# Gated tiles of layer 1 made final in DRAM in paced steps; output stage in another order of heads

## The chip, the cores and the metric

The kernel runs on one core of a Trainium2 chip. Its time is the device time of one execution in microseconds (us); the time of a kernel is the median of its runs. A profile is one execution taken apart by the hardware profiler. TensorE (PE) multiplies matrices, VectorE (DVE), ScalarE (ACT) and GpSimd (POOL) work on tiles, and SyncE (SP) issues most of the DMAs, in the order of its queue.

## What is computed

A decoder trunk of two layers on 1024 tokens of width 1024. Layer 0 is retention, layer 1 differential attention with 16 heads. In each, a branch of width 2048 is gated and projected back to 1024 columns, normalized and added. For the change only the end of layer 1 matters:

```python
attn = probs[:, :, 0] - lam * probs[:, :, 1]          # per head, causal, with a relative bias
out  = einsum('bhqk,bhke->bhqe', attn, v)             # 16 heads of 128 columns
out  = rmsnorm(out, subln_g, eps=GN_EPS) * (1.0 - lambda_init)   # over the 128 columns of a head
y    = out.transpose(0, 2, 1, 3).reshape(B, S, 2048)
gated = silu(g) * y
x    = x + rmsnorm(gated @ w_out, post_norm_g)        # w_out: 2048 x 1024
```

So each output row of a head is scaled by one number, its 1/rms over the head's 128 columns.

## The kernel before

Tokens are in eight blocks of 128. Every matrix product is done as three products of a high and a low part (names with h and l), which is why each matmul line stands three times. A tile that feeds TensorE is therefore made in steps: a load from DRAM (raw), a cast on ScalarE (h), a subtraction of the cast from the original (l) on VectorE or GpSimd.

**Attention of layer 1** walks through 16 heads x 8 query blocks in 128 steps. In between, a stream of filler matmuls (projections of later heads, whose weights `load_w` loads through SP's queue into two raw buffers and splits with ScalarE and GpSimd, line 83) fills TensorE. TensorE's order is written by hand there; the other engines' and SP's orders are made by a scheduler from a simulated timeline, and every engine keeps its order. `values` makes the output of a head for two token blocks, multiplied by the gate (heads 0 to 11) but not yet by 1/rms, and ScalarE's queue stores it in the DRAM tensor g1. `square_sum` stores the sums of squares (ssd). `row_scales` turns them, with the softmax sums s0all that TensorE transposes (line 834), into the 1/rms rows rsd. It runs twice: for heads 0 to 11 in head 12, and for heads 12 to 15 at the very end. For the four late heads the gate is stored apart (sgd).

**Output stage of layer 1** (`output_stage`). For each half of the 1024 output columns and each token block, the sixteen heads are accumulated in one PSUM bank: 16 x 3 matmuls of 128x512. A gated tile comes from `gated8` (eight heads) or from the inner `gated` (four heads): load from g1, load of the 1/rms rows spread over the partitions (w_rb, rsb), multiplication on GpSimd (lines 108, 472), cast on ScalarE (111, 475), subtraction on VectorE (112, 476); in the last four heads also the gate (sgl, line 471). WIDE says how many of the four quarters come from `gated8`: two in each half. Blocks 0 and 1 have heads 0 to 11 of the first half done within attention, as filler; blocks 2, 3 and 4 get them while the last scales are made. After the first half of a block, two tiles of the second half's weights are loaded over the slots (`load_out`). In the second half each block's row is normalized, added to x1d and stored.

`rsqrt` is a Newton iteration on VectorE that begins with a shift and a multiplication.

Of the kernel before, what the change touches and what calls it, by code (L numbers as in the profile page):

```python
# [10 lines left out]
F32 = mybir.dt.float32  # L11
F32R = mybir.dt.float32r
I32 = mybir.dt.int32
# [6 lines left out]
P = 128  # L20
T = 1024
# [14 lines left out]
WIDE = ((4, 4), (2, 2))  # L36
# [5 lines left out]
BSPLIT = 12  # L42
# [8 lines left out]
class _Trunk:  # L51
# [7 lines left out]
    def rsqrt(self, out, v, n, tag, np_=P, t=None, hv=None):  # L59
# [35 lines left out]

    def gated8(self, layer, parts):
        nc = self.nc
        gsrc = self.g0 if layer == 0 else self.g1
        raw = self.wp.tile([P, 8, P], F32, tag="raw", name="w_raw", bufs=2)
        rb = self.wp.tile([P, 8, P], F32, tag="raw", name="w_rb", bufs=2) if layer == 1 else None  # L100
# [350 lines left out]
    def output_stage(self, layer, slots, nextR, prologue, head):  # L451
        nc, io = self.nc, self.io
        gsrc = self.g0 if layer == 0 else self.g1
        with ExitStack() as es:
            ptr = self.pool(es, "fpst", PSUM)
            ptr.tile([P, 4, P], F32, tag="T", name="ps_t", bufs=2)
# [3 lines left out]
            def gated(tb, kq):  # L460
                raw = fp.tile([P, 4, P], F32, tag="graw", name="graw", bufs=3)
                nc.sync.dma_start(raw, gsrc[tb, :, kq * 4:kq * 4 + 4, :])
                if layer == 1:
                    rb = fp.tile([P, 4, P], F32, tag="rsb", name="rsb", bufs=2)
                    b, k0 = (0, kq * 4) if kq * 4 < BSPLIT else (1, kq * 4 - BSPLIT)
                    nc.sync.dma_start(rb, self.rsd[b][tb:tb + 1, k0:k0 + 4, :].broadcast_to([P, 4, P]))
                    if kq == 3:
                        n = DH - LATE
                        sg = fp.tile([P, n, P], F32, tag="sgl", name="sgl")
                        nc.sync.dma_start(sg, self.sgd[tb])  # L470
                        nc.vector.tensor_mul(raw[:, 4 - n:, :], raw[:, 4 - n:, :], sg)  # L471
                    nc.gpsimd.tensor_mul(raw, raw, rb)  # L472
# [576 lines left out]
```

## Time and profile before

| | |
|---|---|
| median of 3 runs | 2211.82 us (2211.01 to 2216.42) |
| profiled execution, its own time | 2212.31 us |
| its span | 2210.5 us |
| mean granted TensorE clock | 0.991 |
| busy: PE, DVE, ACT, POOL | 2145.4, 1325.3, 852.8, 471.0 us |
| DMA | 181.30 MB, mean 82 GB/s |

Attention of layer 1 ends at about 2012 us, the output stage of layer 1 at the span's end. A busy TensorE is one whose modelled matmuls overlap without a gap; the granted clock says at which of its two levels it ran (1.0 is 2.4 GHz). A wait is the idle time of an engine before an instruction, with the instruction that released it.

### The profile page before, as it was taken

How to read it: one execution, taken by the hardware profiler on the slowest of the kernel's cores; microseconds unless marked ns; L12 is line 12 of the kernel's file. 1: busy time of each engine (PE TensorE's matmuls, PEld its weight loads, DVE VectorE, ACT ScalarE, POOL GpSimd, SP SyncE). 2: the span in 40 equal slices, each digit the busy share in tenths (PEclk: the TensorE clock that was granted, in tenths of full speed). 3: DMA queues.
4: the chain of work that ended last, by engine and by line, in shares of the span. 5: the costliest groups of instructions: out<-in, count | busy, mean ns of one | idle time of the engine just before them, and what ended most of it. 6: DMA issues, size and time to landing. Idle time of an engine off the chain costs nothing. (4 is left out here: it accounts for less than half of the span.)

```text
span 2210.5 us, 31034 instructions
## 1 busy us (share of the span) xinstructions
PE 2145.4 (97%) x11860; PEld 1798.2 (81%) x11860; DVE 1325.3 (60%) x3158; ACT 852.8 (39%) x1648; POOL 471.0 (21%) x260
## 2 busy tenths in 40 slices
PE   7999999999999999999999999999999999998997
PEld 7888988888897888787888888887887888776775
DVE  5264344344436348556776676676676776774765
ACT  4121221221122333345455554555545565542421
POOL 2322411501521000211111111111111111123651
PEclk9999999999999999999999999999999999999999
DMA  4112212112123544311111111111111111145874
GB/s 165 61 39 74 61 35 68 44 50 72 44 72 95 191 153 171 101 41 39 51 39 32 47 50 39 40 50 39 38 40 42 48 41 39 63 136 183 280 251 158
DMA packets 95430, 181.30 MB, mean 82 GB/s; under 512 B 8433, under 2 KB 50609, under 8 KB 95153
## 3 DMA queue, kind: packets, MB, share of 16 engines
q1 hardware_dynamic: 60368, 162.31, 22.6%
q10 hardware_dynamic: 34912, 17.01, 2.5%
q8 instruction: 93, 1.52, 0.3%
q14 instruction: 57, 0.46, 0.1%
HBM read 151.86 MB, written 30.56 MB: 83 GB/s over the span
## 5 line engine op out<-in xcount | busy, mean ns | idle before, releaser
L83 POOL TENSOR_TENSOR w_l<-w_raw,w_h 128x1024 fp32r<-128x1024 f32 x112 | 271.5, 2429 | 1332.1 <-ACT w_h L82 1325.3
L762 ACT ACTIVATE e<-ps_s,nm 128x896 f32<-128x896 f32 (+7 forms) x256 | 189.8, 742 | 105.4 <-DVE nm L760 93.8
L216 PE MATMUL ps_mm<-RB,w_h 128*128 128x512 f32 x512 | 209.5, 409 | 0.3 <-ACT RB L151 0.3
L158 PE MATMUL ps_mm<-RA,w_h 128*128 128x512 f32 x512 | 203.7, 398 | 1.6 <-DVE sg L427 1.6
L159 PE MATMUL ps_mm<-RA,w_h 128*128 128x512 f32 x512 | 204.9, 400 | 0.0
L217 PE MATMUL ps_mm<-RB,w_h 128*128 128x512 f32 x512 | 201.9, 394 | 1.0 <-DVE RB L152 1.0
L218 PE MATMUL ps_mm<-RB,w_l 128*128 128x512 f32 x512 | 202.7, 396 | 0.0
L160 PE MATMUL ps_mm<-RA,w_l 128*128 128x512 f32 x512 | 202.3, 395 | 0.0
L789 ACT CAST ath<-ps_t 128x512 fp32r<-128x512 f32 (+1 forms) x192 | 91.8, 478 | 217.3 <-PE ps_t L786 211.9
L757 DVE TENSOR_REDUCE mx<-ps_s 128x1 f32<-128x640 f32 (+2 forms) x192 | 119.4, 622 | 82.3 <-PE ps_s L732 78.0
L82 ACT CAST w_h<-w_raw 128x1024 fp32r<-128x1024 f32 x112 | 117.6, 1050 | 121.0 <-PE ps_mm L159 33.4
L648 PE MATMUL ps_mm<-w_h,RB 128*128 128x256 f32 x512 | 147.7, 289 | 0.0
L170 PE MATMUL ps_mm<-w_h,RA 128*128 128x256 f32 x512 | 145.8, 286 | 0.0
L168 PE MATMUL ps_mm<-w_h,RA 128*128 128x256 f32 x512 | 145.0, 285 | 0.8 <-ACT RA L151 0.8
L169 PE MATMUL ps_mm<-w_l,RA 128*128 128x256 f32 x512 | 145.1, 284 | 0.1
L650 PE MATMUL ps_mm<-w_h,RB 128*128 128x256 f32 x512 | 143.8, 281 | 0.0
L649 PE MATMUL ps_mm<-w_l,RB 128*128 128x256 f32 x512 | 143.8, 281 | 0.0
L111 ACT CAST g_h<-w_raw 128x1024 fp32r<-128x1024 f32 x50 | 52.5, 1049 | 183.8 <-POOL w_raw L108 81.1
L158 PEld LDWEIGHTS ps_mm<-RA,w_h 128*128 128x128 f32 x512 | 96.2, 188 | 25.2 <-DVE sg L427 2.3
L218 PEld LDWEIGHTS ps_mm<-RB,w_l 128*128 128x128 f32 x512 | 96.2, 188 | 23.6
L112 DVE TENSOR_TENSOR g_l<-w_raw,g_h 128x1024 fp32r<-128x1024 f32 x50 | 71.3, 1427 | 73.0 <-ACT g_h L111 71.0
L160 PEld LDWEIGHTS ps_mm<-RA,w_l 128*128 128x128 f32 x512 | 96.2, 188 | 22.0
(217 smaller groups left out, 5520.9 us busy)
## 6 DMA issues: line engine op xcount, KB each, us to landing
w_raw<-in_wn SPq DMA_DIRECT2D x64, 512.0 KB
w_raw<-g SPq DMA_DIRECT2D x48, 512.0 KB
w_raw<-in_wv SPq DMA_DIRECT2D x32, 512.0 KB
w_raw<-in_wo SPq DMA_DIRECT2D x32, 512.0 KB
xt<-in_x SPq DMA_DIRECT2D x16, 512.0 KB
w_raw<-in_wg SPq DMA_DIRECT2D x16, 512.0 KB
g<-go ACTq DMA_DIRECT2D x32, 256.0 KB
g<-go ACTq DMA_DIRECT2D x64, 128.0 KB
```

Of the source, the lines that this page charges most:

```text
L83: nc.gpsimd.tensor_sub(l, raw, _f32(h))
L158: nc.tensor.matmul(ps, wh[:, k], region[:, kt, cols], start=(kt == 0), stop=False)
L159: nc.tensor.matmul(ps, wh[:, k], region[:, 8 + kt, cols], start=False, stop=False)
L160: nc.tensor.matmul(ps, wl[:, k], region[:, kt, cols], start=False, stop=(kt == KT - 1))
L168: nc.tensor.matmul(ps, region[:, kt, cols], wh[:, k], start=(kt == 0), stop=False)
L169: nc.tensor.matmul(ps, region[:, kt, cols], wl[:, k], start=False, stop=False)
L170: nc.tensor.matmul(ps, region[:, 8 + kt, cols], wh[:, k], start=False, stop=(kt == KT - 1))
L216: nc.tensor.matmul(ps, wh[:, k], HR[:, kt, tok], start=(kt == 0), stop=False)
L217: nc.tensor.matmul(ps, wh[:, k], HR[:, 8 + kt, tok], start=False, stop=False)
L218: nc.tensor.matmul(ps, wl[:, k], HR[:, kt, tok], start=False, stop=(kt == KT - 1))
L648: nc.tensor.matmul(ps[:, t, :], HR[:, kt, cols], wh[:, k], start=(kt == 0), stop=False)
L762: nc.scalar.activation(e[:, 0:n], S[:, 0:n], AF.Exp, bias=nm, accum_out=(s0 if m == 0 else s1))
```

## The change

Heads are now in three batches (0 to 7, 8 to 11, 12 to 15), each with its own DRAM tensors for the unscaled tiles (g1r), the sums and the scales; `row_scales` runs at heads 8, 12 and the end. After each of the first two, eight steps later, `finish` takes one quarter of a token block per attention step: it loads the unscaled tile and its scale rows through SP, multiplies on GpSimd, and the next step stores the final tile in g1f. That is 16 + 8 = 24 steps. A scheduling dependency ties their DMAs to a transpose of the step. In the output stage tiles of heads 0 to 11 are loaded final. The last four heads are finished there in the first half, by the old way, and stored for the second half. The first half now goes over heads 0 to 11 of all blocks in pairs, then over heads 12 to 15 of all blocks; six PSUM banks instead of four hold the sums. The second half takes all tiles from `gated8`. In `rsqrt` two lines change places.

```diff
-WIDE = ((4, 4), (2, 2))
+WIDE = ((4, 4), (2, 4))
-BSPLIT = 12
+BATCHES = ((0, 8), (8, 12), (12, 16))
...
+        nc.vector.tensor_scalar(out.bitcast(I32), v.bitcast(I32), 1, None, op0=ALU.arith_shift_right)
         nc.vector.tensor_scalar(hv, v, -0.5, None, op0=ALU.mult)
-        nc.vector.tensor_scalar(out.bitcast(I32), v.bitcast(I32), 1, None, op0=ALU.arith_shift_right)
...
+    def gsrc(self, layer, tb, kt, n):
+        if layer == 0:
+            return self.g0[tb, :, kt:kt + n, :]
+        return self.g1f[kt // 8][tb, :, kt % 8:kt % 8 + n, :]
...
         for tb, kt, n in parts:
-            nc.sync.dma_start(raw[:, o:o + n, :], gsrc[tb, :, kt:kt + n, :])
-            if layer == 1:
-                nc.sync.dma_start(rb[:, o:o + n, :], self.rsd[0][tb:tb + 1, kt:kt + n, :].broadcast_to([P, n, P]))
+            nc.sync.dma_start(raw[:, o:o + n, :], self.gsrc(layer, tb, kt, n))
             o += n
-        if layer == 1:
-            nc.gpsimd.tensor_mul(raw, raw, rb)
...
-            def gated(tb, kq):
+            def gated(tb, kq, hf):
                 raw = fp.tile([P, 4, P], F32, tag="graw", name="graw", bufs=3)
-                nc.sync.dma_start(raw, gsrc[tb, :, kq * 4:kq * 4 + 4, :])
-                if layer == 1:
+                if layer == 1 and kq == 3 and hf == 0:
+                    nc.sync.dma_start(raw, self.g1r[2][tb])
+                    sg = fp.tile([P, 4, P], F32, tag="sgl", name="sgl")
+                    nc.sync.dma_start(sg, self.sgd[tb])
                     rb = fp.tile([P, 4, P], F32, tag="rsb", name="rsb", bufs=2)
...
+                    nc.sync.dma_start(rb, self.rsd[2][tb:tb + 1].broadcast_to([P, 4, P]))
+                    nc.vector.tensor_mul(raw, raw, sg)
                     nc.gpsimd.tensor_mul(raw, raw, rb)
+                    nc.sync.dma_start(self.gsrc(1, tb, 12, 4), raw)
+                else:
+                    nc.sync.dma_start(raw, self.gsrc(layer, tb, kq * 4, 4))
...
-                return psm.tile([P, 512], F32, tag="mm", name="ps_mm", bufs=4)
+                return psm.tile([P, 512], F32, tag="mm", name="ps_mm", bufs=4 if layer == 0 else 6)
...
+                for tb in range(2, TB, 2):
+                    two = (tb, tb + 1)
+                    g = [self.gated8(1, ((t, 0, 8),)) for t in two]
+                    head += [bank() for t in two]
+                    for t in two:
+                        for _ in self.out_mm(head[t], g[t - tb], slots[0], 0, 8):
+                            pass
+                    g8 = self.gated8(1, tuple((t, 8, 4) for t in two))
+                    for t in two:
+                        for _ in self.out_mm(head[t], g8, slots[0], 8, 4, 4 * (t - tb)):
+                            pass
+                    second_half(tb - 2)
+                second_half(TB - 2)
+                for tb in range(TB):
                     product(head[tb], 0, tb, 3)
                     first(tb, head[tb])
+                lead = TB
...
+            def after(dma):
+                self.tc.add_manual_dep(dma.ins, mark["pe"].ins.name, mybir.DependencyInfo(mybir.DependencyClass.NoSync, mybir.DependencyReason.DATA), reason="paced")
+
+            def finish_store():
+                if held:
+                    dst, raw = held.pop()
+                    after(nc.sync.dma_start(dst, raw))
+
+            def finish(tb, h0):
+                b, hh, nh = batch(h0)
+                finish_store()
+                raw = wk.tile([P, 4, P], F32, tag="fraw", name="fraw")
+                rb = wk.tile([P, 4, P], F32, tag="frb", name="frb")
+                after(nc.sync.dma_start(raw, self.g1r[b][tb, :, hh:hh + 4, :]))
+                after(nc.sync.dma_start(rb, self.rsd[b][tb:tb + 1, hh:hh + 4, :].broadcast_to([P, 4, P])))
+                nc.gpsimd.tensor_mul(raw, raw, rb)
+                held.append((self.gsrc(1, tb, h0, 4), raw))
...
                 if rows is not None:
                     row_scales(*rows)
+                    todo += [None] * 8 + [(tb, h0) for h0 in range(*BATCHES[rows[0]], 4) for tb in range(TB)] + [()]
                     rows = None
+                elif todo:
+                    step = todo.pop(0)
+                    if step:
+                        finish(*step)
+                    elif step == ():
+                        finish_store()
```

Three places of the built orders show what moved. The first is SP's queue around heads 9 and 10, where weights (w_raw) for the filler are loaded; bt is a head's bias. Before:

```order
L79 DMA w_raw_15246<-in_wn1 128x1024
L79 DMA w_raw_15398<-in_wn1 128x1024
L79 DMA w_raw_15586<-in_wn1 128x1024
L716 DMA bt_15751<-xd_89 128x256
L79 DMA w_raw_15683<-in_wn1 128x1024
L79 DMA w_raw_15885<-in_wn1 128x1024
```

After, from the first of the same weight loads on (g1r0 holds the unscaled tiles of heads 0 to 7, g1f0 the final ones):

```order
L79 DMA w_raw_15321<-in_wn1 128x1024
L731 DMA fraw_14543<-g1r0_80 128x512
L732 DMA frb_14544<-rsd0_90 128x512
L724 DMA g1f0_83<-fraw_14543 128x512
L732 DMA frb_14612<-rsd0_90 128x512
L731 DMA fraw_14611<-g1r0_80 128x512
L79 DMA w_raw_15485<-in_wn1 128x1024
L724 DMA g1f0_83<-fraw_14611 128x512
L732 DMA frb_14710<-rsd0_90 128x512
L731 DMA fraw_14709<-g1r0_80 128x512
L724 DMA g1f0_83<-fraw_14709 128x512
```

Between two weight loads there now stand the stores and loads of finishing steps; a store waits for GpSimd's multiplication, and the next load of fraw for that store, since fraw has one buffer.

The second is SP's queue in the second half of the output stage, one token block's worth (w_raw is an 8-head tile, w_rb, rsb its scales, graw a 4-head tile, sgl the late gate, xt the residual). Before:

```order
L103 DMA w_raw_20434<-g1_80 128x1024
L462 DMA graw_20364<-g1_80 128x512
L470 DMA sgl_20389<-sgd_82 128x512
L105 DMA w_rb_20435<-rsd12_85 128x1024
L466 DMA rsb_20387<-rsd4_86 128x512
L466 DMA rsb_20469<-rsd12_85 128x512
L564 DMA out_0<-xt_20019 128x512 x2
L103 DMA w_raw_20537<-g1_80 128x1024
L462 DMA graw_20385<-g1_80 128x512
L546 DMA xt_20225<-x1d_81 128x1024
```

After:

```order
L106 DMA w_raw_20409<-g1f1_84 128x1024
L548 DMA xt_20291<-x1d_85 128x1024
L106 DMA w_raw_20464<-g1f0_83 128x1024
L566 DMA out_0<-xt_20206 128x512 x2
L106 DMA w_raw_20494<-g1f1_84 128x1024
```

A token block's eight loads, xt among them, are three, and what is loaded is multiplied by no scale any more.

The third is ScalarE in the last steps of head 15 (e is an exponential of the softmax, ath the copy of a transposed tile that the product with v needs, g_h the cast of a gated tile for the output stage). Before:

```order
L762 ACTIVATE e_19185,s0all_7687<-ps_s_19164,nm_19181 128x768
L808 ACTIVATE sq_19214<-ps_o_19207 128x256
L809 CAST sqh_19215<-sq_19214 128x256
L820 DMA g1_80<-go_19220 128x2x128
L762 ACTIVATE e_19192,s1_19179<-ps_s_19165,nm_19188 128x768
L111 CAST g_h_19347<-w_raw_19342 128x1024
L789 CAST ath_19071<-ps_t_19240 128x4x128
L789 CAST ath_19071<-ps_t_19253 128x2x128
```

After:

```order
L785 ACTIVATE e_19346,s0all_7693<-ps_s_19325,nm_19342 128x768
L110 CAST g_h_19505<-w_raw_19503 128x1024
L831 ACTIVATE sq_19375<-ps_o_19368 128x256
L785 ACTIVATE e_19353,s1_19340<-ps_s_19326,nm_19349 128x768
L832 CAST sqh_19376<-sq_19375 128x256
L844 DMA g1r12_82<-go_19381 128x2x128
L812 CAST ath_19232<-ps_t_19401 128x4x128
L110 CAST g_h_19562<-w_raw_19559 128x1024
L812 CAST ath_19232<-ps_t_19414 128x2x128
```

The cast that stood before both ath copies now stands between them, and it is that of a later tile.

## Rows read from the trace of the kernel before

**Rows 1.** Stretches: bounds, length, busy us (instructions) by engine, PEclk, DMA share, GB/s.
```profile
960.00:1900.00 940.00, 930.23 (x5518) 779.33 (x5517) 659.09 (x1758) 493.14 (x1058) 139.14 (x57) 1.00 0.14 43
...
2034.00:2060.00 26.00, 21.59 (x79) 16.61 (x80) 12.27 (x11) 8.17 (x12) 14.04 (x9) 0.85 0.83 258
```

**Rows 2.** Line 834, TensorE: min/median/max ns, first and last start us, forms.
```profile
L834 PE MATMUL ps_t<-ident,s0all x2: 270/292/313, 1752.7 to 2012.7; 128*96 128x128 f32 x1, 128*32 128x128 f32 x1
```

**Rows 3.** Timeline of TensorE in the output stage: start us, us, engine, line, operation.
```profile
2048.01 0.40 PE L125 MATMUL ps_mm<-RB,gl 128*128 128x512 f32 x1
...
2052.68 0.40 PE L124 MATMUL ps_mm<-RB,gh 128*128 128x512 f32 x1
...
2058.19 0.63 PE L124 MATMUL ps_mm<-RB,gh 128*128 128x512 f32 x1
2058.62 0.63 PE L125 MATMUL ps_mm<-RB,gl 128*128 128x512 f32 x1
...
2201.76 0.39 PE L125 MATMUL ps_mm<-RA,gl 128*128 128x512 f32 x1
```

**Rows 4.** Waits of TensorE, 2012 to 2211: us in total, times, longest.
```profile
PE ps_mm L125 <- DVE gl L476: 14.3, 8, 4.1
PE ps_mm L123 <- ACT g_h L111: 2.8, 1, 2.8
```

**Rows 5.** GpSimd by line, 2012 to 2211: busy us, mean ns, idle before, releasers.
```profile
L472 POOL TENSOR_TENSOR graw<-graw,rsb 128x512 f32<-128x512 f32 x28 | 41.8, 1506 | 47.1 <-DVE nv L559 16.7 <-DVE graw L471 14.8 <-DMA rsb<-rsd 6.0
L108 POOL TENSOR_TENSOR w_raw<-w_raw,w_rb 128x1024 f32<-128x1024 f32 x13 | 32.4, 2492 | 43.0 <-DMA w_rb<-rsd 37.3 <-DVE gl L476 5.0 <-DMA graw<-g 0.7
```

**Rows 6.** VectorE by line, 2012 to 2211.
```profile
L471 DVE TENSOR_TENSOR graw<-graw,sgl 128x512 f32<-128x512 f32 x16 | 22.1, 1382 | 44.6 <-DMA graw<-g 40.4 <-DMA sgl<-sgd 2.4 <-issue 1.8
L112 DVE TENSOR_TENSOR g_l<-w_raw,g_h 128x1024 fp32r<-128x1024 f32 x13 | 20.6, 1585 | 5.7 <-ACT g_h L111 5.7
```

**Rows 7.** Chain that ended last: start us, us, piece (DMA: issue to landing).
```profile
2027.91 1.85 DMA rsd<-rsr
2029.78 3.24 DMA rsb<-rsd
...
2047.18 6.91 DMA graw<-g
...
2096.77 7.74 DMA w_rb<-rsd
...
2184.19 2.08 DMA out<-xt
```

**Rows 8.** Timeline at the end of attention, ScalarE and TensorE; in brackets the wait.
```profile
2003.01 1.05 ACT L111 CAST g_h<-w_raw 128x1024 fp32r<-128x1024 f32 x1 [3.79 <-POOL w_raw L108]
...
2005.98 0.44 PE L786 MATMUL ps_t<-ident,e 128*128 128x128 f32 x2 [1.66 <-DVE atl L790]
```

**Rows 9.** Waits of TensorE in the attention, 960 to 1900.
```profile
PE ps_t L786 <- DVE e L768: 4.4, 6, 1.7
PE ps_o L801 <- DVE nm L760: 1.8, 3, 0.8
PE ps_t L834 <- DVE atl L790: 1.4, 1, 1.4
```

**Rows 10.** GpSimd by line in the attention, 960 to 1900.
```profile
L83 POOL TENSOR_TENSOR w_l<-w_raw,w_h 128x1024 fp32r<-128x1024 f32 x57 | 139.1, 2443 | 816.1 <-ACT w_h L82 816.1
```

**Rows 11.** Timeline in the attention, SP's queue and GpSimd.
```profile
1485.04 19.63 SPq L79 DMA_DIRECT2D w_raw<-in_wn  x3
...
1501.92 2.39 POOL L83 TENSOR_TENSOR w_l<-w_raw,w_h 128x1024 fp32r<-128x1024 f32 x1 [12.77 <-ACT w_h L82]
```

**Rows 12.** Timeline at the end of attention, GpSimd and VectorE.
```profile
1981.04 2.40 POOL L108 TENSOR_TENSOR w_raw<-w_raw,w_rb 128x1024 f32<-128x1024 f32 x1 [5.59 <-DVE mx L759]
1981.18 2.54 DVE L810 TENSOR_TENSOR sql<-sq,sqh 128x256 fp32r<-128x256 f32 x1
...
1997.76 0.42 DVE L810 TENSOR_TENSOR sql<-sq,sqh 128x256 fp32r<-128x256 f32 x1
```

More of the change, by code (lines that the diff above doesn't have):

```diff
@@ L484, in product, with second_half @@
                     return
-                for _ in self.out_mm(ps, gated(tb, kq), slots[hf], kq * 4, 4):
+                for _ in self.out_mm(ps, gated(tb, kq, hf), slots[hf], kq * 4, 4):
                     pass
             def bank():
-                return psm.tile([P, 512], F32, tag="mm", name="ps_mm", bufs=4)
+                return psm.tile([P, 512], F32, tag="mm", name="ps_mm", bufs=4 if layer == 0 else 6)
             acc = {}
+            def second_half(t0):
+                for t in (t0, t0 + 1):
+                    self.load_out(layer, slots, 1, t, fp.tile([P, D], F32, tag="x", name="w_raw", bufs=2))
             def first(tb, ps):
@@ L504, in first @@
                 nc.vector.tensor_mul(acc["y"][:, tb, :], ps, acc["postg"][:, 0:512])
-                if tb % 2 == 0:
-                    for t in (tb, tb + 1):
-                        self.load_out(layer, slots, 1, t, fp.tile([P, D], F32, tag="x", name="w_raw", bufs=2))
+                if layer == 0 and tb % 2 == 0:
+                    second_half(tb)
             if layer == 0:
@@ L708, in batch @@
             def batch(h):
-                return (0, h, BSPLIT) if h < BSPLIT else (1, h - BSPLIT, DH - BSPLIT)
+                return next((b, h - h0, h1 - h0) for b, (h0, h1) in enumerate(BATCHES) if h < h1)
             bts = {}
+            held = []
+            mark = {}
+            def after(dma):
[13 more added lines that the diff above has]
+                held.append((self.gsrc(1, tb, h0, 4), raw))
             def load_bias(h):
@@ L785, in attn_t @@
                 for kb in range(k0, k1):
-                    nc.tensor.transpose(out=tp[:, kb - k0, :], in_=A[:, kb * P:(kb + 1) * P], identity=self.ident)
+                    mark["pe"] = nc.tensor.transpose(out=tp[:, kb - k0, :], in_=A[:, kb * P:(kb + 1) * P], identity=self.ident)
                 clk["pe"] += (k1 - k0) * 0.109
@@ L896, in attention_layer @@
                     ready_o = clk["pe"] + SLACK["sq"]
-                    if i == ORDER[-1] and h == BSPLIT - 1:
+                    if i == ORDER[-1] and h + 1 in (BATCHES[0][1], BATCHES[1][1]):
                         fill_until(ready_o)
@@ L900, in attention_layer @@
                         pend = None
-                        rows = (0,)
+                        rows = (batch(h)[0],)
                 n_ = s + 1
@@ L910, in attention_layer @@
                 square_sum(*pend)
-            row_scales(1)
+            assert not todo and not held
+            row_scales(2)
             return heads
@@ L930, in run @@
         self.g0 = self.dr.tile([TB, P, NE, P], F32, name="g0")
-        self.g1 = self.dr.tile([TB, P, NE, P], F32, name="g1")
+        self.g1r = [self.dr.tile([TB, P, h1 - h0, P], F32, name="g1r%d" % h0) for h0, h1 in BATCHES]
+        self.g1f = [self.dr.tile([TB, P, 8, P], F32, name="g1f%d" % k) for k in range(2)]
         self.x1d = self.dr.tile([T, D], F32, name="x1d")
         self.sgd = self.dr.tile([TB, P, DH - LATE, P], F32, name="sgd")
-        self.ssd = [self.dr.tile([TB, n, P], F32, name="ssd%d" % n) for n in (BSPLIT, DH - BSPLIT)]
-        self.rsd = [self.dr.tile([TB, n, P], F32, name="rsd%d" % n) for n in (BSPLIT, DH - BSPLIT)]
+        self.ssd = [self.dr.tile([TB, h1 - h0, P], F32, name="ssd%d" % h0) for h0, h1 in BATCHES]
+        self.rsd = [self.dr.tile([TB, h1 - h0, P], F32, name="rsd%d" % h0) for h0, h1 in BATCHES]
         a, b = (lambda i: RA[:, i, :]), (lambda i: RB[:, i, :])
```

41 lines of the change are left out of this document (9 added, 32 removed).

## The prediction

> **What bounds the kernel now.** I read the stretches by engine first [rows 1]. In the attention of layer 1 (960 to 1900 us) TensorE is busy for 930 of 940 us at full granted clock: nothing can be won there, and everything added there must stay hidden. In the output stage it loses ground: from 2034 us it is busy for 21.6 of 26 us, at a granted clock of 0.85, with a DMA share of 0.83. So that is the place to look at.
>
> How much is there to win? The stage has 8 blocks x 2 halves x 16 heads x 3 = 768 matmuls. 72 of them (blocks 0 and 1, heads 0 to 11, first half) are done in the attention; 696 follow the transposition of line 834 at 2012.7 us [rows 2]. Undisturbed they start 0.234 us apart (20 steps from 2048.01 to 2052.68) [rows 3]: 696 x 0.234 = 162.9 us. The last ends at 2201.76 + 0.39 = 2202.15 [rows 3], after 189.4 us. **26.5 us are lost.** The waits name most of them: 14.3 us in 8 waits for gl and 2.8 us for g_h [rows 4]. The rest comes behind such waits: after the longest, the matmuls start 0.43 us apart (2058.19, 2058.62) [rows 3], which is TensorE at the lower of its two levels, 1.2 instead of 2.4 GHz.
>
> Why does gl come late? Every gated tile is loaded, its 1/rms rows are loaded beside it (rsb, w_rb), GpSimd multiplies, ScalarE casts, VectorE subtracts; and each tile is made twice, once for each half of the output columns. GpSimd alone spends 41.8 + 32.4 us on that after 2012 us, and stands 37.3 us before w_rb [rows 5]. VectorE stands 40.4 us at line 471, in its order, until graw lands [rows 6].
>
> **The second half (384 matmuls).** All tiles now come final from DRAM. Gone per token block are two rsb loads, one w_rb, one sgl and two graw, three GpSimd multiplications and one VectorE multiplication; left are two 8-head tiles, xt and the output. A tile serves 24 matmuls, 5.6 us. Making one takes a load of at most 7.74 us [rows 7], a cast of 1.05 us [rows 8] and a subtraction of 1.59 us [rows 6]: 10.4 us, over two raw buffers 5.2 us a tile, even in before's traffic. I expect no wait here.
>
> **The first half (312 matmuls after 2012.7).** TensorE has 216 matmuls (heads 0 to 11 of blocks 2 to 7), 50.5 us, before it needs the last scales, at about 2063 us. They are in DRAM at 2027.91 + 1.85 = 2029.8 us [rows 7]. If the VectorE work that now stands inside their chain (a weight subtraction, a tile, a product) adds 5 us, 28 us are still spare. What is late next is the last four heads: eight blocks of 12 matmuls, 2.8 us each. sgl has a single buffer there, so a block costs at least a load of 3.24 to 6.91 us [rows 7] and a multiplication of 1.38 us [rows 6]: 4.6 to 8.3 us. The order has the first four sgl loads ahead of TensorE's arrival. The other four fall behind by 4 x 1.8 to 4 x 5.5 = 7.2 to 22 us, less the three blocks that three graw buffers hold ready, 8.4 us. That gives 0 to 13.6 us; I take **+3**, near the low end, since the traffic behind the 6.91 us is what the change removes.
>
> **End of attention.** ScalarE, in order, stood 3.79 us in front of the cast at 2003.01 until GpSimd's multiplication was done, and TensorE lost 1.66 us at 2005.98 behind it [rows 8]. The multiplication is gone, and the cast now stands behind the first of the two ath copies; but it still stands before the last one and waits there for TensorE to free a buffer. Bounds -4 (this wait, the slow matmuls behind it, and a like wait before) and +2; I take **-2**.
>
> **A third pass over the scales,** at head 8. The pass at head 12 shows a TensorE wait of 1.4 us [rows 9]. Bounds 0 and 3; I take **+1.5**.
>
> **The 24 paced steps** put 72 DMAs on SP's queue and 24 multiplications on GpSimd's, in order, before weight loads and w_l subtractions of heads 8 to 14. GpSimd first: in 940 us it spent 139.1 us on 57 subtractions [rows 10], and TensorE's three longest rows of waits for VectorE are 4.4 + 1.8 + 1.4 = 7.6 us [rows 9]. If all of it came from GpSimd, 24 x 1.5 us [rows 5] = 36 us more cost 36 x 7.6 / 139.1 = 2 us. I take **+2**, bounds 0 and 6. Now SP. A step is a store, the loads, a multiplication, in series: 2.08 + 3.24 [rows 7] + 1.5 [rows 5] + 1 us for three issues = 7.8 us, or 11.5 us with a load of 6.91. Attention goes on by a step in (2012.7 - 1752.7) / 32 = 8.1 us (the two dates of line 834 lie 32 steps apart [rows 2]). So SP just keeps up. What hides a delay: the load issued at 1485.04 is subtracted at 1501.92 [rows 11], 16.9 us later; less at most 6 us to land and 1.05 us of cast, 10 us are spare for a weight tile. I cost the queue at nothing.
>
> VectorE and GpSimd hinder each other: sql, 0.42 us at 1997.76, took 2.54 us at 1981.18, beginning 0.14 us after a GpSimd multiplication and ending when that had ended [rows 12]. The Trainium skill ("SBUF — State Buffer", section "SBUF: two separate sides") has the rule for it: the port pair that the two engines share is an exclusive lock, held for a whole instruction, if the VectorE operation reads two SBUF inputs. The trace agrees in this row. By that rule the change carries the lock into the softmax, at worst 24 times; that case is the third rival below.
>
> **Layer 0** differs by two VectorE lines of rsqrt that changed places; the scheduler then orders some retention matmuls otherwise. 0, bounds -2 and +2.
>
> **Sum.** -26.5 + 3 - 2 + 1.5 + 2 = -22.0 us. Against the profiled execution's own 2212.31 us (span 2210.5) this is 2190.3 us; that execution lies 0.5 us above the median of 2211.82, so **2190 us**.
>
> **Rivals.** (1) The output stage stays bound by its feed. For it: the DMA share of 0.83 [rows 1], the single sgl buffer, VectorE's standing in its order before graw [rows 6]. The far end of the last four heads costs 13.6 instead of 3 us: 2201 us. Against it: most loads of scales and products are gone. (2) The step chain on SP is too slow, and weight tiles come late. At 10.1 us a step the sixteen steps of the first batch fall behind by 16 x 2.0 = 32 us; less the 10 us spare TensorE loses 22 us, the gain is gone: 2212 us. From 10.5 us a step on (16 x 2.4 - 10 = 28) the kernel is over 0.3% slower than before; at 11 us it takes 2226 us. Against it: the long loads were measured at 258 GB/s, attention moves 43 GB/s [rows 1]. (3) Each new GpSimd multiplication pushes the softmax by its 1.5 us, and TensorE with it: 36 instead of 2 us, 2224 us. Against it: 57 longer ones cost at most 7.6 us. (4) The change does less than it says: the added scheduling dependency on a transpose leaves no wait of SP on TensorE in the built order, so steps may bunch. SP then runs them as fast as its queue allows, one after another between weight loads; that costs nothing by itself, and its bad end is rival 2.
>
> **Chances.** The forecast, 2182 to 2197 us: 0.70. Rival 1, 2197 to 2204: 0.15. Better than 2182 (all terms at their good ends): 0.04. Rival 2 at about 10 us a step, no change: 0.06; beyond 10.5 us: 0.03. Rival 3: 0.02. A difference under 0.3%, 6.6 us, can't be told from none. Faster 0.89, same 0.06, slower 0.05. The range leaves out the better end, rivals 2 and 3: **2182 to 2204 us**.
>
> **What would show it.** In the profile after: no waits for gl or g_h in the first 50 us of the output stage and in its second half, and a granted clock of 1.0 there; the last four heads with waits of a few us in all, for gl, in blocks 4 to 7; finishing steps about 8 us apart or less and no TensorE wait for w_h or w_l in heads 8 to 14; the last matmul about 22 us earlier. Waits for w_h or w_l would show rival 2; more waits for nm, e or atl in heads 8 to 14, rival 3; long waits for gl late in the first half, rival 1. Each would make the prediction wrong.

## The result, and the profile after

The changed kernel takes **2182.3 us** (median of 4 runs, 2179.4 to 2183.9) against 2212.8 us before (4 runs beside them): ratio 0.9859, 95% interval 0.9842 to 0.9876, a gain of 30 us by the medians and 31 by the ratio. Run again later it took 2182.35 us (2181.7 to 2185.0), ratio 0.9861 (0.9845 to 0.9877). The forecast was 2190 us, a gain of 22. The direction and the main place were right; 8 to 9 us of the gain were not foreseen, and the time lies at the low end of the range, or by the ratio (0.9859 x 2211.82 = 2180.6 us) just below it.

The profiled execution of after took 2179.38 us (span 2177.6), which is 3 us below its median; before's lay at its own. The top of the page, busy time and share by engine:

```profile
PE 2132.8 (98%) x11861; PEld 1790.8 (82%) x11861; DVE 1283.4 (59%) x3155; ACT 851.6 (39%) x1638; POOL 429.3 (20%) x246
```

**The output stage** did what was forecast. Stretches in after (bounds, length, busy us by engine, PEclk, DMA share, GB/s), to be held against the second of [rows 1]:

```profile
2030.00:2060.00 30.00, 30.00 (x130) 24.16 (x129) 15.60 (x14) 11.77 (x14) 14.77 (x7) 1.00 0.87 293
2060.00:2090.00 30.00, 27.95 (x118) 21.57 (x118) 13.39 (x19) 8.29 (x21) 4.54 (x3) 1.00 0.45 139
2090.00:2120.00 30.00, 30.00 (x130) 24.16 (x129) 17.28 (x47) 7.90 (x12) 0.00 (x0) 1.00 0.49 168
```

TensorE is busy without a gap from 2030 to 2060 us and in the second half, at the full granted clock, although the DMA share is higher than before in the first of these stretches (0.87). All its waits there, 2003.5 to 2178, in answer to [rows 4]:

```profile
PE ps_mm L124 <- DVE gl L475: 2.0, 3, 1.3
PE ps_mm L122 <- DVE rsr L860: 0.6, 1, 0.6
```

The 2.0 us for gl stand in the last four heads (2060 to 2090), as the prediction said, and are all that is left of 14.3.

**But the stage also begins 9.4 us earlier.** The transposition that [rows 2] dates 2012.7 now comes at 2003.3 (line 857, three instead of two since the scales go in three passes):

```profile
L857 PE MATMUL ps_t<-ident,s0all x3: 270/285/297, 1486.7 to 2003.3; 128*32 128x128 f32 x2, 128*64 128x128 f32 x1
```

To find where those 9.4 us come from, I dated a landmark that both kernels have 64 times, VectorE's copy of ssr after each pair of attention steps (line 824 before, 848 after). From copy to copy the two traces can be laid side by side:

| stretch | before, us | after, us | difference |
|---|---|---|---|
| start of the span to 1st copy (layer 0, first head) | 992.77 | 991.26 | -1.5 |
| 1st to 31st copy | 485.91 | 485.86 | 0.0 |
| 31st to 33rd (the third pass, head 8) | 34.46 | 36.58 | +2.1 |
| 33rd to 58th (where the 24 steps run) | 405.59 | 403.76 | -1.8 |
| 58th to 60th | 30.56 | 31.28 | +0.7 |
| 60th to 64th (the end of attention) | 63.60 | 54.79 | **-8.8** |
| 64th to the end of the span (output stage) | 197.61 | 174.07 | **-23.5** |

The sum is -32.9 us, the difference of the spans. The output stage gives 23.5, which is what the prediction had for it (26.5 less 3). The end of attention gives 8.8 where it had 2. That stretch in before, with the same columns as above:

```profile
1949.29:2012.89 63.60, 53.72 (x264) 41.68 (x263) 42.15 (x98) 26.21 (x56) 17.20 (x7) 0.95 0.39 120
```

And in after:

```profile
1948.74:2003.53 54.79, 49.56 (x263) 38.96 (x261) 42.12 (x100) 27.58 (x57) 5.50 (x2) 1.00 0.37 118
```

TensorE runs the same instructions (264 and 263), but stands 53.72 - 49.56 = 4.2 us less long on them (granted clock 1.00 instead of 0.95) and idles 5.2 instead of 9.9 us, 4.6 less. GpSimd is the engine that lost work: 5.50 instead of 17.20 us. Six multiplications of line 108 are gone; what is left are subtractions of output weights (line 94).

### The profile page after: what moved, and what is told of

It is laid out like the page before. It is cut to its first block, busy times and chain, and to the rows that moved or that the text cites. A ratio compares the mean times of both kernels' runs of the same rounds, so it can differ in the third digit from the quotient of the medians.

```text
span 2177.6 us, 31046 instructions
## 1 busy us (share of the span) xinstructions
PE 2132.8 (98%) x11861; PEld 1790.8 (82%) x11861; DVE 1283.4 (59%) x3155; ACT 851.6 (39%) x1638; POOL 429.3 (20%) x246
## 4 chain that ended last, share of the span: by engine, by line
PE 92%; DVE 3%; issue 1%; ACT 1%; DMA 1%; POOL 0%; ACTq 0%; DVEq 0%; POOLq 0%
PE ps_mm L158 6%; PE ps_mm L157 6%; PE ps_mm L159 5%; PE ps_mm L215 5%; PE ps_mm L122 5%; PE ps_mm L124 5%; PE ps_mm L123 5%; PE ps_mm L217 5%; PE ps_mm L216 5%; PE ps_t L809 3%; PE ps_ret L396 3%; PE ps_s L752 3%; PE ps_mm L650 3%; PE ps_mm L651 3%; PE ps_mm L652 3%; PE ps_mm L167 3%
## 5 line engine op out<-in xcount | busy, mean ns | idle before, releaser
L111 DVE TENSOR_TENSOR g_l<-w_raw,g_h 128x1024 fp32r<-128x1024 f32 x60 | 82.7, 1378 | 105.7 <-ACT g_h L110 105.6
L110 ACT CAST g_h<-w_raw 128x1024 fp32r<-128x1024 f32 x60 | 63.0, 1051 | 172.2 <-PE ps_mm L123 126.4
```

## The experiments

All times are medians; ratios are against the kernel before, run on the same chip. "The stretch" is the 60th to the 64th copy of ssr.

### Is it GpSimd's multiplication? (before, without it)

```diff
-        if layer == 1:
-            nc.gpsimd.tensor_mul(raw, raw, rb)
         gh = self.wp.tile([P, 8, P], F32R, tag="wh", name="g_h", bufs=3)
```

> The kernel before without GpSimd's multiplication of the 8-head tiles of layer 1 by 1/rms (it leaves that scaling of heads 0 to 11 out where 8-head tiles are made); the loads of w_rb stay. Measure: the time from the fifth last copy of ssr to the last one, 63.6 us in before (1949.29 to 2012.89), 54.8 in after (1948.74 to 2003.53). Theory A, GpSimd's multiplications cost it (they stop VectorE, and ScalarE's cast stands behind them): 54 to 57 us. Theory B, the loads of w_rb and graw's company on the queues cost it, or the order of the tiles: 62 to 64 us. For the whole kernel A gives 2193 to 2205 us (8 us in the attention and up to 10 in the output stage, where 13 more of them go), B about 2212 less what the output stage gains, 2203 to 2212.

Measured: 2199.1 us, ratio 0.9939 (0.9923 to 0.9956); the stretch takes 54.60 us:

```profile
1951.93:2006.53 54.60, 49.32 (x264) 39.24 (x263) 39.82 (x99) 27.13 (x57) 3.11 (x1) 1.00 0.48 154
```

Theory A, and B is out: with w_rb still loaded (DMA share even 0.48) the stretch is as short as in after. Nothing else of the change is needed for these 9 us. In the output stage, where 13 more of these multiplications go, the gain is only 3.5 us (194.07 us from the last copy to the end, against 197.61), where up to 10 were expected.

### What of it costs: that VectorE is stopped, or that a cast waits? (before, product written aside)

```diff
-            nc.gpsimd.tensor_mul(raw, raw, rb)
+            nc.gpsimd.tensor_mul(rb, raw, rb)
```

> The kernel before with the same multiplication, of the same size, but its result written into w_rb, where nobody reads it (so the tile stays unscaled): VectorE meets it as before, ScalarE's cast no longer waits for it. Same measure, 63.6 us in before and 54.8 in after. Theory A1, GpSimd's multiplication costs by stopping VectorE while it runs: 60 to 64 us. Theory A2, it costs by the cast that stands in ScalarE's order until it is done (1.78, 4.23 and 3.79 us of waiting at 1983.47, 1992.80 and 2003.01): 55 to 58 us. Between them (58 to 60) both share it. The whole kernel: A1 2205 to 2212, A2 2195 to 2204 us.

Measured: 2209.3 us, ratio 0.9984 (0.9973 to 0.9994); the stretch takes 63.40 us:

```profile
1948.84:2012.24 63.40, 53.89 (x264) 42.42 (x263) 46.42 (x99) 25.93 (x56) 17.59 (x7) 0.92 0.41 132
```

A1. ScalarE no longer waits for GpSimd at all (10.2 us in 4 waits before), and the stretch is 0.2 us shorter, no more. VectorE shows why: busy 46.42 us, 6.6 more than without the product, for the same 99 instructions. Its longest ones and a multiplication beside them, from the timeline:

```profile
1957.60 2.12 DVE L766 SCALAR_TENSOR_TENSOR arr<-arr,neglam,s0all 128x1 f32<-128x1 f32 x1
...
1977.69 2.39 POOL L108 TENSOR_TENSOR w_rb<-w_raw,w_rb 128x1024 f32<-128x1024 f32 x1 [4.51 <-DMA w_rb<-rsd]
...
1977.85 2.25 DVE L766 SCALAR_TENSOR_TENSOR arr<-arr,neglam,s0all 128x1 f32<-128x1 f32 x1
```

The arr line works on a single column and takes 0.22 us elsewhere. Here it begins 0.16 us after the multiplication and ends 0.02 us after it. Before the change VectorE was busy for 42.15 us there, so it is stopped more often once the cast waits no longer; that the one cost takes the other's place is my reading of these two numbers. So the run shows that the stops alone can cost as much; how the two share the price in before is read from before's own trace, in the section on the prediction.

### Put back into after

```diff
+        if layer == 1 and self.again > 0:
+            self.again -= 1
+            nc.gpsimd.tensor_mul(raw, raw, _f32(self.ones).unsqueeze(1).broadcast_to([P, 8, P]))
         gh = self.wp.tile([P, 8, P], F32R, tag="wh", name="g_h", bufs=3)
```

(self.again begins at 6.)

> The changed kernel with one GpSimd multiplication by ones put back ahead of the cast in the first six 8-head tiles of layer 1 (those made in the attention), without the loads of w_rb. Same measure, 54.8 us in after, 63.6 in before. Theory A: it goes back to 59 to 64 us, and the kernel takes 2186 to 2192 us. Theory B (loads, traffic, order): 54 to 56 us, and the kernel stays at 2182 within 2 us.

Measured: 2189.5 us, ratio 0.9896 (0.9882 to 0.9911), 7.2 us over after; the stretch takes 63.21 us:

```profile
1948.19:2011.40 63.21, 54.47 (x263) 42.09 (x261) 48.05 (x100) 29.01 (x58) 17.45 (x8) 0.92 0.34 105
```

Theory A again: 8.4 us come back with the multiplications and no load (five of the six stand in the stretch, the first ends as it begins; from the 58th copy, with all six, it is 6.7 us). ScalarE shows no wait for GpSimd here, while VectorE is busy for 48.05 us instead of 42.12: in this kernel it is the stops that cost, not a cast that waits. One of the meetings in the timeline, where e of one 128x128 block, 0.34 us in before at 1986.76, ends 0.15 us after GpSimd does:

```profile
1984.86 2.34 POOL L110 TENSOR_TENSOR w_raw<-w_raw,ones 128x1024 f32<-128x1024 f32 x1
...
1985.18 2.17 DVE L794 SCALAR_TENSOR_TENSOR e<-e,arr 128x128 f32<-128x128 f32 x1
```

### The same place, but GpSimd reads nothing

Moving an instruction moves others: the scheduler placed some casts and subtractions otherwise in each of these kernels. So the last one was run once more with two memsets in place of the multiplication (the text below calls that kernel "the run before last").

```diff
-            nc.gpsimd.tensor_mul(raw, raw, _f32(self.ones).unsqueeze(1).broadcast_to([P, 8, P]))
+            nc.gpsimd.memset(raw, 1.0)
+            nc.gpsimd.memset(raw, 1.0)
```

> The run before last with GpSimd's work put back ahead of the first six casts, but as two memsets of the tile in place of the multiplication (they overwrite the tile with ones, so heads 0 to 11 of blocks 0 to 3 are left out of the result). All instructions of TensorE, ScalarE and SyncE stand in the same order as with the multiplication, VectorE's but for four rows; the casts wait for GpSimd again. What is gone is that GpSimd reads SBUF. Measure: fifth last to last copy of ssr, 54.8 us in after, 63.2 with the multiplication. Theory A1, the two engines stop each other, and only where GpSimd reads: 54.5 to 57 us, the kernel 2181 to 2184. Theory A2, the cast standing in order behind GpSimd, or the order itself: 60 to 64 us, 2187 to 2191. If the memsets are much shorter than 2.4 us together, A2 is tested less hard by that share.

Measured: 2182.5 us, ratio 0.9858 (0.9844 to 0.9873); the stretch takes 57.16 us:

```profile
1947.80:2004.96 57.16, 51.39 (x263) 40.03 (x261) 42.01 (x100) 29.02 (x58) 14.93 (x12) 0.97 0.38 116
```

A1, a little over the upper end. The twelve memsets take 11.4 us (1.9 us a tile) where the six multiplications took 14.5 (2.4 us each), so GpSimd's time is tested less hard by a fifth. ScalarE shows no wait for GpSimd, as in the run with the multiplication. VectorE passes the memsets unhindered:

```profile
1985.64 0.48 DVE L795 SCALAR_TENSOR_TENSOR e<-e,arr 128x256 f32<-128x256 f32 x1
...
1985.74 0.95 POOL L110 MEMSET w_raw<- 128x1024 f32 x1 [1.52 <-DMA w_raw<-g1f]
...
1986.12 1.23 DVE L115 TENSOR_TENSOR g_l<-w_raw,g_h 128x1024 fp32r<-128x1024 f32 x1
1986.75 0.95 POOL L111 MEMSET w_raw<- 128x1024 f32 x1
```

The 60th copy itself shifts a little from kernel to kernel, so here are the four runs by a longer measure too:

| kernel | 60th to 64th copy, us | 58th to 64th copy, us |
|---|---|---|
| before | 63.6 | 94.2 |
| before, no product | 54.6 | 86.5 |
| before, product aside | 63.4 | 94.4 |
| after | 54.8 | 86.1 |
| after, product put back | 63.2 | 92.8 |
| after, memsets in its place | 57.2 | 86.2 |

By the first the memsets leave 2.4 of the 8.4 us to the order and to GpSimd's time, by the second 0.1 of 6.7. What costs is that GpSimd reads SBUF while VectorE works. The Trainium skill ("SBUF — State Buffer", section "SBUF: two separate sides") says that a VectorE operation with two SBUF inputs is locked out only against a GpSimd operation that reads SBUF; the last two rows agree.

### What the order of the output stage is worth (after, with the order of before)

```diff
-                for tb in range(2, TB, 2):
+                for tb in (2,):
...
+                lead = 5
+                head.append(bank())
+                for kq in range(3):
+                    product(head[4], 0, 4, kq)
+                for tb in range(lead):
                     product(head[tb], 0, tb, 3)
                     first(tb, head[tb])
-                lead = TB
```

> The changed kernel, tiles finished in the attention as there, but the first half of the output stage in the order of before: heads 0 to 11 of blocks 0 to 4 first, then their last four heads, then blocks 5 to 7 whole. TensorE then reaches the last four heads after 3 x 36 = 108 matmuls, 25 us, not after 216, 50 us. Measure: from the last copy of ssr to the end of the span, 197.6 us in before (2012.89 to 2210.5), 174.1 in after (2003.53 to 2177.6). Theory: the order is worth what the late scales and the sgl loads need: 182 to 192 us, the kernel 2190 to 2200. Rival: once the tiles are final the order is worth nothing, 174 to 176 us, 2181 to 2185.

Measured: 2189.7 us, ratio 0.9895 (0.9880 to 0.9910). From the last copy of ssr (2005.66) to the end of the span 182.6 us, at the low end of what the theory gave. The waits of TensorE in the stage:

```profile
PE ps_mm L124 <- DVE gl L475: 6.6, 2, 4.0
PE ps_mm L122 <- DVE rsr L861: 0.6, 1, 0.6
```

And its stretch of 2030 to 2060, where the granted clock falls behind those waits:

```profile
2030.00:2060.00 30.00, 23.42 (x88) 18.11 (x87) 15.11 (x16) 9.71 (x17) 8.69 (x5) 0.89 0.77 259
```

So of the 23.5 us that the stage gained, 197.6 - 182.6 = 15.0 come with the final tiles and 182.6 - 174.1 = 8.5 with heads 0 to 11 of all blocks first.

### What the pace is worth (after, steps not tied to TensorE)

```diff
             def after(dma):
-                self.tc.add_manual_dep(dma.ins, mark["pe"].ins.name, ...)
+                pass
```

> The changed kernel without the pacing: the loads and stores of the 24 finishing steps don't wait for TensorE's transposition, everything else is the same. Theory P, the pace matters: SP runs ahead, the steps bunch, their loads and GpSimd multiplications stand before weight loads and weight subtractions; TensorE shows waits for w_h, w_l, or more for e, nm and atl in heads 8 to 14, and the kernel takes 2185 to 2195 us. Rival, my prediction's fourth case: it costs nothing, 2180 to 2184 us, and the steps' multiplications stand elsewhere but do no harm.

Measured: 2197.7 us, ratio 0.9929 (0.9914 to 0.9943): half of the gain is gone. Theory P, and by more than its range. The steps' multiplications now come 7.1 us apart (1502.87 to 1609.12 for the first sixteen) against 8.7 us in after (1558.33 to 1688.44). The 33rd to 58th copy of ssr take 416.3 us instead of 403.8. The first loss in the timeline, on SP's queue, ScalarE and TensorE:

```profile
1549.57 0.32 SPq L731 DMA_DIRECT2D fraw<-g1r  x1
1549.99 0.38 SPq L79 DMA_DIRECT2D w_raw<-in_wv  x1
...
1555.66 1.05 ACT L82 CAST w_h<-w_raw 128x1024 fp32r<-128x1024 f32 x1 [5.87 <-DMA bt<-xd]
...
1560.94 0.48 PE L809 MATMUL ps_t<-ident,e 128*128 128x128 f32 x1 [3.98 <-DVE atl L813]
```

The same load and cast in after:

```profile
1536.04 0.33 SPq L79 DMA_DIRECT2D w_raw<-in_wv  x1
...
1549.21 1.05 ACT L82 CAST w_h<-w_raw 128x1024 fp32r<-128x1024 f32 x1 [0.77 <-PE ps_mm L609]
```

The weight load is issued 14 us later by these dates, 12.6 when the later start of this execution (first copy of ssr at 992.65 against 991.26 us) is taken off; seven finishing steps have gone ahead of it. Its cast stands 5.87 us at the head of ScalarE's queue (the releaser named, bt, is the transfer issued just behind the weights), and in that queue sq and ath of the softmax stand behind it. So TensorE's wait reads "atl", and no row reads w_h: a late weight shows at whoever is queued behind its cast. This is rival 2's mechanism, on a smaller step time than the prediction asked of it.

### Where else the end of attention loses (after, output weights' subtractions on VectorE)

In after one meeting is left in the stretch, GpSimd's subtraction of an output weight over a sql that takes 0.42 us elsewhere:

```profile
1977.86 2.39 POOL L94 TENSOR_TENSOR RB<-w_raw,RB 128x1024 fp32r<-128x1024 f32 x1 [8.47 <-ACT RB L92]
...
1978.12 2.41 DVE L833 TENSOR_TENSOR sql<-sq,sqh 128x256 fp32r<-128x256 f32 x1
```

```diff
-        eng = nc.vector if (t % 2 == 0) else nc.gpsimd
+        eng = nc.vector if t % 2 == 0 or (layer, hf) == (1, 0) else nc.gpsimd
```

> The changed kernel with GpSimd's subtractions of the output weights of the first half (line 94, every second one) on VectorE, so that GpSimd does nothing in the last two steps of the attention. In after one of them, 2.39 us at 1977.86, lies over a VectorE sql that took 2.41 instead of 0.42 us (1978.12). Measure: fifth last copy of ssr to the last, 54.8 us in after. If what remains there is GpSimd stopping VectorE: 52 to 53.5 us, the kernel 2179 to 2181. If VectorE's own load counts (1.23 us more for each subtraction moved): 54.5 to 57 us, 2182 to 2185.

Measured: 2180.1 us, ratio 0.9852 (0.9837 to 0.9867), not to be told from after. The stretch takes 54.82 us, at the low end of the second theory, while the time lies in the range of the first: what VectorE gains by not being stopped it spends on the subtractions (busy 41.78 us there against 42.12). Only the 58th to 60th copy come closer together (29.95 instead of 31.28 us).

### The third pass (after, scales in two passes)

```diff
-BATCHES = ((0, 8), (8, 12), (12, 16))
+BATCHES = ((0, 12), (12, 16))
...
-                    todo += [None] * 8 + [(tb, h0) for h0 in range(*BATCHES[rows[0]], 4) for tb in range(TB)] + [()]
+                    todo += [None] * 3 + [(tb, h0) for tb in range(TB) for h0 in range(*BATCHES[rows[0]], 4)] + [()]
```

> The changed kernel with the scales in two passes (heads 0 to 11, 12 to 15) as before, so without the pass at head 8; the 24 finishing steps then run from head 13 on, block by block. By the copies of ssr the third pass costs 2.1 us (after's lead over before falls from 1.56 us at the 31st to -0.56 at the 33rd). If that is all: the 33rd copy comes 2.1 us earlier against the 31st (34.5 instead of 36.6 us), the end of attention is as in after, and the kernel takes 2179 to 2181 us. Rival: the steps, squeezed into the last three heads, meet the weights, the softmax and the first 8-head tiles there, and the end of the attention gives it back: fifth last to last copy of ssr 57 to 64 us instead of 54.8, the kernel 2183 to 2190.

Measured: 2191.7 us, ratio 0.9900 (0.9884 to 0.9917). Both sentences came true, and the time lies a little above the rival's range. The 31st to 33rd copy take 34.04 us, 2.5 less than in after: that is the third pass. The rest gives it back and more: 61.41 us for the stretch, and before it 35.5 instead of 31.3. ScalarE's waits in the stretch:

```profile
ACT g_h L110 <- DMA w_raw<-g1f: 4.9, 1, 4.9
```

The first 8-head tiles now come behind the last finishing steps. The third pass buys the time in which the tiles are finished out of the way.

### Three small repairs together, and two of them

> The changed kernel with three things that the traces of after show: line 94's subtractions of the first half on VectorE (as in the run above); sgl in a ring of three buffers with rsb instead of one of its own (2.0 us of waits for gl in the last four heads); the passes over the scales after the filler that follows the transposition, not straight behind it (two waits of 1.4 us for atl, and 2.5 us lost at head 8). If each gives what its wait shows: 1.3 + 1.5 + 3 = 5 to 6 us, 2176 to 2178. If the waits only move: 2179 to 2183.

("The run above" is the one with line 94 on VectorE.)

Its two edits beside the one on line 94 (the ring and the place of the pass):

```diff
-                    sg = fp.tile([P, 4, P], F32, tag="sgl", name="sgl")
+                    sg = fp.tile([P, 4, P], F32, tag="rsb", name="sgl", bufs=3)
-                    rb = fp.tile([P, 4, P], F32, tag="rsb", name="rsb", bufs=2)
+                    rb = fp.tile([P, 4, P], F32, tag="rsb", name="rsb", bufs=3)
...
+                    fill_until(t_done + SLACK["turn"])
                     row_scales(*rows)
+                    t_done = clk["pe"]
```

Measured: 2183.3 us, ratio 0.9863 (0.9848 to 0.9877): no gain, a miss for the first theory. The ring holds (0.8 us of waits for gl instead of 2.0, 172.9 us from the last copy to the end). The pass at head 8 gains 1.4 us on after by the 34th copy, but the one at head 12 loses 4.5 us between the 48th and the 49th, in one wait:

```profile
PE ps_t L809 <- DVE atl L813: 5.2, 1, 5.2
```

The trace shows why it is that long. Two weight subtractions of GpSimd lie over two steps of the pass's Newton iteration, which take 0.3 us otherwise and stand in VectorE's order before atl:

```profile
1756.15 4.71 POOL L83 TENSOR_TENSOR w_l<-w_raw,w_h 128x1024 fp32r<-128x1024 f32 x2 [28.40 <-ACT w_h L82]
...
1756.22 2.44 DVE L73 TENSOR_TENSOR rss<-rss,rsv 32x128 f32<-32x128 f32 x1
...
1758.92 2.08 DVE L74 SCALAR_TENSOR_TENSOR rsr<-rss,rsr 32x128 f32<-32x128 f32 x1
```

With the pass left where it was:

> The changed kernel with two of the three edits of the run before last but one: line 94's subtractions of the first half on VectorE, and sgl in one ring of three buffers with rsb; the passes over the scales stay where the change has them. Output stage (last copy of ssr to the end of the span): 172.9 us with the ring against 174.1 in after. VectorE's subtractions gave the attention 1.2 us between the 58th and the 64th copy. If both hold together: 2178 to 2181 us against 2182.3. If what is gained in the attention is given back: 2181 to 2184. A difference under 3 us can't be told from none by the intervals; then the dates in the trace are all that speaks for it.

("The run before last but one" is the one just shown.) Measured: 2179.2 us (5 runs, 2178.1 to 2181.5), ratio 0.9847 (0.9831 to 0.9863). No wait for gl is left; 173.0 us from the last copy to the end. It is the fastest by its median, 3 us below after, but the intervals overlap widely, so it can't be called faster than the change.

### Layer 0

> The kernel before with nothing changed but the two VectorE lines of rsqrt, which change places as in the change. The trace of after is 1.5 us ahead of before's at the first copy of ssr in layer 1 (991.26 against 992.77 us) and keeps that lead until head 7. If the swap is the cause, by the order of the layer-0 matmuls that follows from it, the first copy of ssr comes at 991.3 us here (990.9 to 991.7) and the last at 2011.4. If the lead comes from anything else, it comes at 992.8 and 2012.9. The time itself can't tell 1.5 us: 2210 to 2213 by either.

```diff
-        nc.vector.tensor_scalar(hv, v, -0.5, None, op0=ALU.mult)
         nc.vector.tensor_scalar(out.bitcast(I32), v.bitcast(I32), 1, None, op0=ALU.arith_shift_right)
+        nc.vector.tensor_scalar(hv, v, -0.5, None, op0=ALU.mult)
```

Measured: 2211.6 us (one run); first copy of ssr at 994.23, last at 2013.24. Neither theory's date: no lead shows. How far the first copy spreads the other runs show. The changed kernel again:

> The changed kernel again, unchanged, to be compared with the run above on one chip: 2180 to 2184 us. Its first copy of ssr in layer 1 comes within 991 to 995 us: the other runs so far spread it over 991.3 to 994.4, though layer 0 is the same.

Measured: 2182.35 us, first copy at 992.20. Over all profiled executions the first copy lies between 991.3 and 994.4 us, with before's layer 0 (992.8 to 993.9) as with after's (991.3 to 994.4). Most of that spread arises in two places of layer 0, where the granted clock fell in some executions and not in others. At one of them TensorE is busy just as long in after and in the run without pacing, but gets through 103 matmuls in the one and 96 in the other:

```profile
905.00:930.00 25.00, 23.16 (x103) 18.09 (x102) 11.74 (x27) 10.42 (x17) 4.80 (x2) 1.00 0.19 63
905.00:930.00 25.00, 23.16 (x96) 18.06 (x95) 10.59 (x24) 10.17 (x16) 4.10 (x2) 0.93 0.18 56
```

The other lies between 690 and 720 us (1.00 or 0.94). Executions with neither fall have their first copy at 991.3 to 992.8 us, those with one at 992.6 to 993.9, those with both at 994.2 and 994.4; the swapped kernel had both. So the lead of 1.5 us can't be told from this spread, and whether the swap is worth a part of it stays open.

## Why the prediction was wrong by 9 us

**Right: the output stage.** 23.5 us by forecast (26.5 less 3) and by measurement. Step by step: no wait for g_h, none for gl in the second half or the first 50 us; the granted clock 1.00; the feed of the last four heads 2.0 us of waits, near the low end taken. Rival 1 did not happen, though the DMA share (0.87) was as high as before: the load on the queues was not the bound. From TensorE's transposition to its last matmul the stage took 166.4 us (2003.3 to 2169.7), 3.5 over the undisturbed 162.9 where the sum had 3. That the order matters by 8.5 us the run with the old order shows.

**Wrong: the term "end of attention", -2 with bounds -4 and +2.** It measured -8.8 us (-8.1 from the 58th copy). The step that failed is the one that priced GpSimd's multiplications there. It counted one way in which they cost, the cast that ScalarE holds until one is done [rows 8], with TensorE's 1.66 us behind it, slow matmuls and "a like wait before". The other way, a VectorE instruction that is stopped, it put at nothing. The trace of before has six multiplications of 2.4 us in that stretch, and both ways. Two stop VectorE, the one of [rows 12] and this one:

```profile
1950.84 2.36 POOL L108 TENSOR_TENSOR w_raw<-w_raw,w_rb 128x1024 f32<-128x1024 f32 x1 [3.98 <-DMA w_rb<-rsd]
...
1950.94 2.67 DVE L768 SCALAR_TENSOR_TENSOR e<-e,arr 128x384 f32<-128x384 f32 x1
...
1953.75 0.52 PE L786 MATMUL ps_t<-ident,e 128*128 128x128 f32 x3 [1.81 <-DVE e L768]
```

e takes 0.62 us in after (1950.96), here 2.67, and TensorE loses 1.81 us; behind the sql of [rows 12] it loses 0.72 (1984.59). Two hold a cast, the one of [rows 8] and the like one before:

```profile
1990.39 2.38 POOL L108 TENSOR_TENSOR w_raw<-w_raw,w_rb 128x1024 f32<-128x1024 f32 x1 [6.95 <-DMA w_rb<-rsd]
...
1992.80 1.05 ACT L111 CAST g_h<-w_raw 128x1024 fp32r<-128x1024 f32 x1 [4.23 <-POOL w_raw L108]
...
1995.90 0.39 PE L801 MATMUL ps_o<-atl,RA 128*128 128x256 f32 x1 [1.35 <-DVE nm L760]
```

Behind the other two (1962.03 and 2009.69) TensorE shows at most a wait of 0.52 us (1969.23). And its clock fell to the lower level behind the waits that the two held casts made, nowhere else in the stretch:

```profile
1949.29:1994.00 44.71, 39.70 (x204) 30.24 (x202) 33.29 (x79) 20.45 (x44) 11.90 (x5) 1.00 0.40 121
1997.00:2001.50 4.50, 4.50 (x14) 3.51 (x14) 2.51 (x8) 1.67 (x4) 1.47 (x1) 0.62 0.23 83
2006.00:2012.00 6.00, 4.44 (x22) 4.08 (x22) 1.19 (x4) 1.16 (x3) 2.31 (x1) 0.72 0.32 93
```

So 2.5 us of waits behind stopped VectorE instructions were missing, and the part that was counted was too small: 3.0 us of waits behind the casts and 4.2 us of slower instructions, where the bound allowed 4 for all of it. These 9.7 us are a little more than the 8.8 that came back; after has a wait of its own there, 1.24 us behind the sql that line 94 stops. The fall of the clock is not this one execution's: the kernel with the swapped lines, which has the same multiplications, took 63.83 us at 0.95, and six executions of after and its variants that leave this stretch calm took 54.3 to 55.1 at 1.00. [rows 12] had shown the stop, and the prediction used it as a danger that the change brings (rival 3), not as a cost that it takes away. The runs price all six multiplications together at 6.7 to 8.4 us when put back and 7.6 to 9.0 when taken out, by the two measures; that is 1.1 to 1.5 us each on average, and by the trace of before four of them carry it.

**The third pass:** +1.5, inside its bounds; measured 2.1 against before (34.46 us) and 2.5 against the run with two passes (34.04).

**The 24 paced steps:** +2, measured 0. The 33rd to 58th copy take 403.6 to 405.4 us in the runs with paced steps as in after, 404.1 to 405.7 in those without any. Both spread by about 1.5 us, for TensorE's clock fell between the 40th and the 41st copy in some executions (last section): without that fall it is 403.6 to 403.8 with the steps and 404.1 without, with it 405.0 to 405.4 and 405.6 to 405.7. Rival 3 did not happen: the steps' multiplications take 1.29 us, and in the middle of the attention nothing of their cost shows, while those of 2.4 us at its end cost 1.1 to 1.5 each. Why one place forgives what the other doesn't was not tested.

**SP's queue** at nothing: right for the paced kernel: TensorE has no wait for weights, and the cast at 1549.21 finds its load landed. But the reason given, that a step of 7.8 us just fits into 8.1, was not the one that carries. Unpaced steps are faster (7.1 us) and cost 15 us. What counts is which loads stand behind the steps in SP's order at the moment a weight buffer comes free: the load was 12.6 us late, its cast 5.1 (both less the later start), and TensorE lost 4.0. The 10 us that the prediction called spare were some 7.5 here.

**Rival 4** had its premise right and its consequence wrong. In after, from 1500 to 1960 us, SP shows no wait for TensorE; its steps wait for GpSimd and for their own stores, and the weight loads between them for GpSimd's subtraction:

```profile
SPq L79 <- POOL w_l L83: 218.4, 20, 24.7
SPq L724 <- POOL fraw L733: 67.2, 17, 5.5
SPq L731 <- DMA g1f<-fraw: 43.9, 21, 5.2
```

But the steps don't bunch: the dependency gave them their places in SP's order, between weight loads that themselves come at the pace of the attention. Without it they run in a row, and that isn't free.

**Layer 0:** 0 with bounds of 2 us, and nothing beyond the spread of the executions was seen.

With -8.1 in place of -2, 2.1 in place of 1.5 and 0 in place of +2 the sum is -26.5 + 3 - 8.1 + 2.1 = -29.5 us, 2182.8 us.

## What to carry to other kernels

When a trace shows that two engines stop each other, count it on both sides of the sum: what the change adds, and what it takes away. Price an instruction that holds up a chain by a run without it, or by the sum of what it stretches on the other engine, not by the one wait that its reader shows. And when side work is put on an in-order queue, ask what may stand behind it at each moment: the same work, placed at the pace of the main loop, cost nothing here that could be seen, and left to run in a row 15 us.

## What the runs showed of the hardware

- A GpSimd instruction that reads SBUF stops a VectorE instruction with two SBUF inputs that begins after it, until it ends, however small that one is: arr on 128x1 took 2.25 us instead of 0.22, e on 128x128 2.17 instead of 0.34. Where VectorE began first, GpSimd took longer: 2.95 us at 2000.03 in before, over an e that began at 1999.71 and kept its 1.02 us. A GpSimd memset of the same tile stopped nothing (e 0.48, g_l 1.23 us beside it).
- The first copy of ssr lies at 991.3 to 994.4 us in 14 executions though layer 0 is all but the same: a lead of that size between two traces is no effect.
- Behind the same wait TensorE's clock fell in one execution and not in another. From the 40th to the 41st copy of ssr, before and before with the product aside have the same meeting (e 2.53 us under a subtraction of line 83) and the same wait of TensorE behind it (1.72 us for e), and differ by 1.5 us:

```profile
1619.10:1647.09 27.99, 25.72 (x125) 20.27 (x124) 20.56 (x44) 12.34 (x26) 7.07 (x3) 0.94 0.20 62
1619.68:1646.13 26.45, 24.16 (x125) 19.07 (x124) 20.48 (x44) 12.23 (x26) 7.07 (x3) 1.00 0.22 65
```

The changed kernel took 26.1 us there in one execution (clock 1.00) and 27.5 in another (0.94). So most of the 1.8 us by which after gains between the 33rd and the 58th copy is this fall, and no effect of the change.
